# A PSUM pool of its own for the second layer's attention, with one two-bank score buffer and a lead of two units

## The chip, the cores and the metric

The kernel runs on one core of a Trainium2 chip. The metric is device time in microseconds (us), the median of several runs. One further execution is taken by the hardware profiler; its trace is what is read below. Engines are named as the profile names them: PE is TensorE (PEld its weight loads), DVE VectorE, ACT ScalarE, POOL GpSimd, SP the queue that issues the loads.

## The reference, cut to what matters

A trunk of two layers on x of 512 x 1024 floats. The first is a latent-attention layer with softmax, the second a stick-breaking-attention layer that reads keys and values made from the residual stream after the first. Each layer's mixer output is multiplied by a SiLU gate, projected and added to the stream; then a per-layer embedding, gated by a sigmoid of the stream, is added. The part that the change touches:

```python
def sb_layer(x, k_sh, v_sh, ln_g, w_in, w_out):
    h = rmsnorm(x, ln_g)
    q, gate = jnp.split(h @ w_in, [MIX_WIDTH], axis=-1)
    ...
    o = stick_breaking_attention(q, k_sh, v_sh)
    return x + (o * jax.nn.silu(gate)) @ w_out

# in stick_breaking_attention, for a block of 128 queries:
z = einsum(q, k) * scale
log_one_minus = where(mask, log_sigmoid(-z), 0)
tail = reversed_cumsum(log_one_minus) - log_one_minus
a = where(mask, exp(log_sigmoid(z) + tail), 0)
o = einsum(a, v)
```

The kernel uses products in place of sums of logarithms: sigmoid(z) times the running product of sigmoid(-z).

## The kernel before

Every fp32 operand of a product is split into a rounded high part and the rest, and each product is three TensorE products (`mm3`, L122 to L124). A weight tile is loaded by SP, for the second layer multiplied by norm gains on POOL (L170, L606), its high part cast on ACT (L131), its low part subtracted on DVE or POOL (L132).

PSUM has eight banks of 128 x 512 floats. One pool, `pp`, serves the whole kernel with tags `g` (2 banks), `s` (2), `t` (3) and `o` (1). `gps` takes the bank of a weight product from a string of tags in turn: "gst" for the first group of each layer, "gstt" for the embedding and the output projection, "g" alone while attention runs.

The order of instructions on each engine is drawn up when the kernel is built. A list scheduler goes by a priority number, which is the place in the program unless it is shifted, and by a simulated timeline: of what is ready it takes the lowest number. `hp(offset=...)` moves instructions ahead by so many steps, `pri(self.mp)` moves the products of `gemm_gen` and `sb_group` back by so many. A tag's slots are given out in that order; a tile that finds none free waits for the release of an old one. A pool opened where a closed one lay waits, by default, with all its tiles for every user of the closed one.

The first layer's attention takes 64 units (16 heads, 4 query blocks). `mla_front` makes a unit's scores, and its DVE instruction at L574 writes an SBUF tile of tag `e`; exponential, normalisation (L582, L585) and four units later the transposes (L532, in `pt_evac`) follow, after which the `e` tile is free. The tile of query block 0 is kept until block 1's transposes. The same tag holds the input's eight x tiles and four tiles of `out_ple`.

Between the layers, `out_ple` ends with the gate products of eight chunks, and for each a sigmoid (L744), a product (L746), a sum (L747), its split into the two parts of x2 (L148, L149), a square (L875) and a sum of squares on POOL (L876). From the last sum come eight tiny products (L881), the mean (L884), the power -1/2 (L885), and `row_of`: four transposes (L190) and the copy to R2 (L192).

In the second layer heads go in four groups of four. For each group `sb_group` makes V (four tiles of 24 products of 256 columns), two chunks of K and two of Q (24 products of 512 columns each). While the attention of a group runs, the generator in `windows` makes the next group's, then the SiLU gates (`gate2`).

A pair of heads has three units (u = 0, 1, 2), so there are 24. `sb_scores` writes each head's scores to a bank of its own; the two heads sit on the upper and the lower 64 rows of the array. `sb_front` makes four sigmoids (L648, L653), a scan per head on DVE (L658) and a product per head on POOL (L659). `pt_evac` transposes the result on PE (L532) and copies it out in two parts (L537, L538); after a pair's third unit `av` (L552) multiplies with V. `sb_layer` puts the transposes `lead` units behind the scores.

Of the kernel before, what the change touches and what calls it, by code (L numbers as in the profile page):

```python
# [6 lines left out]
F32 = mybir.dt.float32  # L7
# [3 lines left out]
AF = mybir.ActivationFunctionType  # L11
# [33 lines left out]
SB_LEAD = 1  # L45
# [3 lines left out]
SB_PRIO = (0, 100, 0, 100)  # L49
MLA_FILL = (0, 100)  # L50
SB_FILL = (0, 300)
# [7 lines left out]
SPREAD_PLE = "gstt"  # L59

# [19 lines left out]
def trunk_kernel(tc, A):  # L80
    from contextlib import ExitStack
    with ExitStack() as ctx:
        Trunk(ctx, tc, A).run()


class Trunk:
    def __init__(self, ctx, tc, A):
        self.tc, self.nc, self.A = tc, tc.nc, A
        self.cp = ctx.enter_context(tc.tile_pool(name="cp", bufs=1))
        self.sp = ctx.enter_context(tc.tile_pool(name="sp", bufs=1))  # L90
        self.pp = ctx.enter_context(tc.tile_pool(name="pp", bufs=1, space=PSUM))
        self.dp = ctx.enter_context(tc.tile_pool(name="dp", bufs=1, space=DRAM))
        self.n = 0

    BUFS = {"A": 8, "B": 10, "qk": 8, "hat": 6, "gate": 8, "v": 2, "f": 6, "e": 12, "ws": 3, "wh": 2, "wl": 2, "R": 1,
            "sm": 16, "smg": 3, "g": 2, "s": 2, "t": 3, "o": 1}
# [529 lines left out]
    def sb_scores(self, u, qs, ks):  # L626

        nc = self.nc
        ps = [self.ps([P, S], "s") for _ in range(2)]
        parts = [(1, 0, 2), (0, 2, 2)] if u == 0 else [(u + 1, 0, u + 2)]  # L630
        terms = [(qs[0], ks[0]), (qs[0], ks[1]), (qs[1], ks[0])]
        for j, c0, nb in parts:
            for i, (q, k) in enumerate(terms):
                for hh in range(2):
                    rows = slice(hh * HD, (hh + 1) * HD)
                    nc.tensor.matmul(ps[hh][:, c0 * P:(c0 + nb) * P], lhsT=q[rows, j * P:(j + 1) * P],  # L636
                                     rhs=k[rows, 0:nb * P], start=i == 0, stop=i == 2, tile_position=(hh * HD, 0))
        return ps

    def sb_front(self, u, ps):  # L640


        nc, v = self.nc, self.nc.vector
        n = (3, 3, 4)[u] * P
        mask = self.maskp if u == 0 else self.maskb[:, S - n:S]
        oms, bs = [[self.t([P, S + 8], F32, "e") for _ in range(2)] for _ in range(2)]
        for om, p in zip(oms, ps):
            nc.scalar.activation(om[:, 0:n], p[:, 0:n], AF.Sigmoid, scale=-(HD ** -0.5))  # L648
            v.memset(om[:, n:n + 1], 0.0)
            if u == 0:  # L650
                v.memset(om[:, 2 * P - 1:2 * P], 0.0)
        for b, p in zip(bs, ps):
            nc.scalar.activation(b[:, 0:n], p[:, 0:n], AF.Sigmoid, scale=HD ** -0.5)  # L653
            if u == 0:
                v.memset(b[:, 2 * P - 1:2 * P], 0.0)
        for om, b in zip(oms, bs):
            x = om[:, 0:n][:, ::-1]
            v.tensor_tensor_scan(out=x, data0=x, data1=mask[:, ::-1], initial=0.0, op0=ALU.mult, op1=ALU.max)  # L658
            nc.gpsimd.tensor_tensor(out=b[:, 0:n], in0=b[:, 0:n], in1=om[:, 1:n + 1], op=ALU.mult)  # L659
        return bs  # L660

    def sb_layer(self, windows, pair, lead, off):
# [5 lines left out]
        for i in range(NU * NH // 2 + lead):  # L668
# [13 lines left out]
            if b >= 0:  # L682
                m, u = divmod(b, NU)
                e = bs.pop(b)
                with hp(offset=off[2]):
                    for hh in range(2):
                        self.pt_evac(2 * m + hh, u, e[hh])
# [110 lines left out]
    def run(self):  # L798
# [88 lines left out]
        self.R2 = self.row_of(r2)  # L887
        self.gates, self.outs, self.og = [[None] * NK for _ in range(3)]
# [18 lines left out]
        self.cyc = SPREAD  # L907
# [10 lines left out]
        self.cyc = SPREAD_PLE  # L918
# [63 lines left out]
```

## Time and profile before

| | |
|---|---|
| median of 3 runs | 714.16 us (713.75 to 715.67) |
| the profiled execution | 718.74 us |
| its span, first to last instruction | 717.0 us |
| PE busy | 681.0 us (95%) |
| DVE, ACT, POOL busy | 497.1, 387.8, 364.0 us |
| mean granted clock | 0.98 |

The times of rows are us from the start of the span. A row of a timeline gives start, duration, engine, line and operation, output and inputs; in brackets the engine's idle time before it and what ended that. A busy matmul row includes its passage through the array, so rows overlap: from start to start is the rate. In a windows row the busy times stand in the order PE, PEld, DVE, ACT, POOL, unless it is of one engine; then come the granted clock, the share of the DMA engines and GB/s.

### The profile page before, as it was taken

The page shows a single profiled execution, that of the slowest core. Times are in us where ns is not written, and L with a number is a line of the kernel's source. Part 1 is how long each engine was busy: PE and PEld are TensorE (multiplying, and loading weights), DVE is VectorE, ACT ScalarE, POOL GpSimd, SP SyncE. Part 2 cuts the span into 40 slices and gives each one's busy share as a digit, 9 for nine tenths or more (in the row PEclk, how much of TensorE's full clock was granted, in tenths as well). Part 3 has the DMA queues.
Part 4 walks back from the last instruction along what each step waited for, and adds up shares of the span by engine and source line. Part 5 has one row for each costly group of instructions (what it writes and reads, how often), then busy time and mean ns, then how long its engine had stood idle before and what let it go on. Part 6 is the DMA issues. An engine that isn't in the chain of part 4 may idle for free.

```text
span 717.0 us, 10008 instructions
## 1 busy us (share of the span) xinstructions
PE 681.0 (95%) x3558; PEld 570.6 (80%) x3558; DVE 497.1 (69%) x935; ACT 387.8 (54%) x773; POOL 364.0 (51%) x293
## 2 busy tenths in 40 slices
PE   8799999999988999999799999999999989999997
PEld 6588888878867888887688888877788768888886
DVE  6748499989877865645757787776976987644432
ACT  7256596966986865453343665543563545622321
POOL 6629566754894441038635655545843895200132
PEclk9999999999999999999999999999999999999999
DMA  6242211000014212533322122033012211443231
GB/s 230 67 130 87 79 49 63 30 31 16 16 44 134 89 59 73 159 119 109 128 89 89 51 68 60 1 88 89 30 59 88 89 59 59 161 137 112 75 134 59
DMA packets 21474, 59.29 MB, mean 83 GB/s; under 512 B 2864, under 2 KB 3376, under 8 KB 21424
## 3 DMA queue, kind: packets, MB, share of 16 engines
q1 hardware_dynamic: 21424, 58.65, 25.9%
q8 instruction: 28, 0.46, 0.3%
q14 instruction: 22, 0.18, 0.1%
HBM read 54.45 MB, written 4.19 MB: 82 GB/s over the span
## 4 chain that ended last, share of the span: by engine, by line
PE 59%; DVE 14%; issue 11%; POOL 8%; ACT 6%; DMA 1%; SPq 0%; POOLq 0%; ACTq 0%; DVEq 0%
PE g L122 10%; PE g L124 10%; PE g L123 10%; PE o L552 4%; PE t L122 3%; PE t L124 3%; PE t L123 3%; PE s L122 3%; PE s L123 3%; PE t L532 3%; PE s L124 3%; PE s L636 2%; POOL e L659 2%; DVE wl L132 1%; POOL ws L170 1%
## 5 line engine op out<-in xcount | busy, mean ns | idle before, releaser
L131 ACT CAST wh<-ws 128x1024 fp32r<-128x1024 f32 (+2 forms) x92 | 90.7, 986 | 137.0 <-issue 53.1
L132 DVE TENSOR_TENSOR wl<-ws,wh 128x1024 fp32r<-128x1024 f32 (+2 forms) x72 | 100.1, 1391 | 42.3 <-ACT wh L131 41.9
L122 PE MATMUL g<-A,wh 128*128 128x512 f32 x280 | 113.0, 403 | 9.2 <-ACT wh L331 4.6
L123 PE MATMUL g<-A,wh 128*128 128x512 f32 x280 | 112.2, 401 | 1.6 <-DVE A L149 1.6
L124 PE MATMUL g<-A,wl 128*128 128x512 f32 x280 | 111.2, 401 | 1.2 <-DVE wl L132 0.8
L659 POOL TENSOR_TENSOR e<-e,e 128x384 f32<-128x384 f32 (+1 forms) x48 | 63.3, 1337 | 31.8 <-ACT e L653 11.3
L170 POOL TENSOR_TENSOR ws<-ws,gc 128x1024 f32<-128x1024 f32 x24 | 53.3, 2220 | 51.4 <-DMA ws<-in_w_k 22.7
L122 PEld LDWEIGHTS g<-A,wh 128*128 128x128 f32 x280 | 53.6, 192 | 21.1 <-ACT wh L331 5.7
L537 ACT CAST pth<-t 128x384 fp32r<-128x384 f32 (+1 forms) x96 | 48.4, 525 | 36.5 <-PE t L532 34.3
L538 DVE TENSOR_TENSOR ptl<-t,pth 128x384 fp32r<-128x384 f32 (+1 forms) x96 | 55.4, 591 | 15.9 <-ACT pth L537 15.5
L746 POOL TENSOR_TENSOR f<-f,B 128x512 f32<-128x512 f32 x8 | 14.2, 1773 | 102.1 <-ACT f L744 101.9
L124 PEld LDWEIGHTS g<-A,wl 128*128 128x128 f32 x280 | 53.2, 191 | 13.4 <-DVE wl L132 1.5
L123 PEld LDWEIGHTS g<-A,wh 128*128 128x128 f32 x280 | 53.7, 192 | 12.6 <-DVE A L149 2.0
L532 PE MATMUL t<-ident,e 128*128 128x128 f32 x320 | 55.7, 275 | 7.8 <-POOL e L659 6.6
L132 POOL TENSOR_TENSOR wl<-ws,wh 128x1024 fp32r<-128x1024 f32 (+2 forms) x20 | 41.6, 2079 | 25.1 <-ACT wh L131 24.3
L532 PEld LDWEIGHTS t<-ident,e 128*128 128x128 f32 x320 | 39.0, 140 | 15.2 <-POOL e L659 8.7
L658 DVE TENSOR_TENSOR_SCAN e<-e,maskb 128x384 f32<-128x384 f32 (+1 forms) x32 | 44.7, 1431 | 9.0 <-ACT e L648 8.9
L578 ACT ACTIVATE e<-e,sm,smg 128x128 f32<-128x128 f32 (+1 forms) x64 | 42.1, 660 | 11.6 <-DVE sm L577 11.3
L582 POOL TENSOR_SCALAR e<-e,sm 128x384 f32<-128x384 f32 (+3 forms) x48 | 29.1, 615 | 25.9 <-DVE sm L580 24.4
L552 PE MATMUL o<-pth,v 128*128 128x256 f32 (+2 forms) x128 | 42.1, 340 | 0.0
L552 PE MATMUL o<-ptl,v 128*128 128x256 f32 (+2 forms) x128 | 41.2, 343 | 0.0
L648 ACT ACTIVATE e<-s 128x384 f32<-128x384 f32 (+1 forms) x48 | 23.4, 525 | 31.7 <-PE s L636 31.5
(320 smaller groups left out, 1857.1 us busy)
## 6 DMA issues: line engine op xcount, KB each, us to landing
ws<-in_w_pg SPq DMA_DIRECT2D x16, 512.0 KB, 3.5
ws<-in_w_g SPq DMA_DIRECT2D x8, 512.0 KB, 3.2
ws<-in_w_o SPq DMA_DIRECT2D x16, 256.0 KB, 2.6
ws<-in_w_v SPq DMA_DIRECT2D x8, 512.0 KB, 3.6
ws<-in_w_k SPq DMA_DIRECT2D x8, 512.0 KB, 3.5
ws<-in_w_sq SPq DMA_DIRECT2D x8, 512.0 KB, 3.5
ws<-in_w_sg SPq DMA_DIRECT2D x8, 512.0 KB, 3.5
ws<-in_w_o SPq DMA_DIRECT2D x8, 512.0 KB, 3.5
```

The costliest lines, as they stand in the source:

```text
L122: mm(ps, lhsT=wh, rhs=xh, start=first, stop=False)
L123: mm(ps, lhsT=wh, rhs=xl, start=False, stop=False)
L124: mm(ps, lhsT=wl, rhs=xh, start=False, stop=last)
L131: nc.scalar.copy(out=wh, in_=src)
L132: lo_engine.tensor_tensor(out=wl, in0=src, in1=f32(wh), op=ALU.subtract)
L170: nc.gpsimd.tensor_tensor(out=ws, in0=ws, in1=gain.unsqueeze(2).to_broadcast((P, nk, P)), op=ALU.mult)
L532: nc.tensor.transpose(ps[:, i], src[:, c * P:(c + 1) * P], self.ident)
L537: nc.scalar.copy(out=views[0], in_=ps)
L538: nc.vector.tensor_tensor(out=views[1], in0=ps, in1=f32(views[0]), op=ALU.subtract)
L552: nc.tensor.matmul(ps[:, q0:S], lhsT=V[:, c, hh], rhs=rhs, start=(c == 0 and i == 0), stop=(c == NT - 1 and i == 1))
L658: v.tensor_tensor_scan(out=x, data0=x, data1=mask[:, ::-1], initial=0.0, op0=ALU.mult, op1=ALU.max)
L659: nc.gpsimd.tensor_tensor(out=b[:, 0:n], in0=b[:, 0:n], in1=om[:, 1:n + 1], op=ALU.mult)
```

## The change

The second layer gets a PSUM pool of its own, opened after R2 is made and the first pool closed. Its tags are `g` (2 banks), `t` (3), `o` (1) and `s2`, one buffer of two banks. Both heads' scores are one tile of that tag; the sigmoids take both heads at once, and `e` tiles hold both heads (6 slots of twice the size in place of 12). Scores go two units ahead of transposes. All priority offsets of the layer become zero. Weight products of the layer's first group, of the embedding and of the output projection take banks by "gtt".

```diff
@@ -42,13 +42,13 @@
 
 MLA_LEAD = (4, 4, 2)
 
-SB_LEAD = 1
+SB_LEAD = 2
 
 
 MLA_PRIO = (50, 50, 50, 50)
-SB_PRIO = (0, 100, 0, 100)
+SB_PRIO = (0, 0, 0, 0)
 MLA_FILL = (0, 100)
-SB_FILL = (0, 300)
+SB_FILL = (0, 0)
 
 
 GATES = (4, 1, 1, 2, 0)
@@ -57,6 +57,7 @@
 
 SPREAD = "gst"
 SPREAD_PLE = "gstt"
+SPREAD_SB = "gtt"
 
 
 def _two_pi_parts():
@@ -78,9 +79,10 @@
 
 
 def trunk_kernel(tc, A):
-    from contextlib import ExitStack
     with ExitStack() as ctx:
-        Trunk(ctx, tc, A).run()
+        t = Trunk(ctx, tc, A)
+        with t.pctx:
+            t.run()
 
 
 class Trunk:
@@ -88,12 +90,13 @@
         self.tc, self.nc, self.A = tc, tc.nc, A
         self.cp = ctx.enter_context(tc.tile_pool(name="cp", bufs=1))
         self.sp = ctx.enter_context(tc.tile_pool(name="sp", bufs=1))
-        self.pp = ctx.enter_context(tc.tile_pool(name="pp", bufs=1, space=PSUM))
+        self.pctx = ExitStack()
+        self.pp = self.pctx.enter_context(tc.tile_pool(name="pp", bufs=1, space=PSUM))
         self.dp = ctx.enter_context(tc.tile_pool(name="dp", bufs=1, space=DRAM))
         self.n = 0
 
-    BUFS = {"A": 8, "B": 10, "qk": 8, "hat": 6, "gate": 8, "v": 2, "f": 6, "e": 12, "ws": 3, "wh": 2, "wl": 2, "R": 1,
-            "sm": 16, "smg": 3, "g": 2, "s": 2, "t": 3, "o": 1}
+    BUFS = {"A": 8, "B": 10, "qk": 8, "hat": 6, "gate": 8, "v": 2, "f": 6, "e": 6, "ws": 3, "wh": 2, "wl": 2, "R": 1,
+            "sm": 16, "smg": 3, "g": 2, "s": 2, "t": 3, "o": 1, "s2": 1}
 
     def t(self, shape, dt, tag):
         self.n += 1
@@ -626,14 +629,14 @@
     def sb_scores(self, u, qs, ks):
 
         nc = self.nc
-        ps = [self.ps([P, S], "s") for _ in range(2)]
+        ps = self.ps([P, 2, S], "s2")
         parts = [(1, 0, 2), (0, 2, 2)] if u == 0 else [(u + 1, 0, u + 2)]
         terms = [(qs[0], ks[0]), (qs[0], ks[1]), (qs[1], ks[0])]
         for j, c0, nb in parts:
             for i, (q, k) in enumerate(terms):
                 for hh in range(2):
                     rows = slice(hh * HD, (hh + 1) * HD)
-                    nc.tensor.matmul(ps[hh][:, c0 * P:(c0 + nb) * P], lhsT=q[rows, j * P:(j + 1) * P],
+                    nc.tensor.matmul(ps[:, hh, c0 * P:(c0 + nb) * P], lhsT=q[rows, j * P:(j + 1) * P],
                                      rhs=k[rows, 0:nb * P], start=i == 0, stop=i == 2, tile_position=(hh * HD, 0))
         return ps
 
@@ -643,21 +646,18 @@
         nc, v = self.nc, self.nc.vector
         n = (3, 3, 4)[u] * P
         mask = self.maskp if u == 0 else self.maskb[:, S - n:S]
-        oms, bs = [[self.t([P, S + 8], F32, "e") for _ in range(2)] for _ in range(2)]
-        for om, p in zip(oms, ps):
-            nc.scalar.activation(om[:, 0:n], p[:, 0:n], AF.Sigmoid, scale=-(HD ** -0.5))
-            v.memset(om[:, n:n + 1], 0.0)
-            if u == 0:
-                v.memset(om[:, 2 * P - 1:2 * P], 0.0)
-        for b, p in zip(bs, ps):
-            nc.scalar.activation(b[:, 0:n], p[:, 0:n], AF.Sigmoid, scale=HD ** -0.5)
-            if u == 0:
-                v.memset(b[:, 2 * P - 1:2 * P], 0.0)
-        for om, b in zip(oms, bs):
-            x = om[:, 0:n][:, ::-1]
+        om, b = [self.t([P, 2, S + 8], F32, "e") for _ in range(2)]
+        nc.scalar.activation(om[:, :, 0:n], ps[:, :, 0:n], AF.Sigmoid, scale=-(HD ** -0.5))
+        nc.scalar.activation(b[:, :, 0:n], ps[:, :, 0:n], AF.Sigmoid, scale=HD ** -0.5)
+        v.memset(om[:, :, n:n + 1], 0.0)
+        if u == 0:
+            for x in (om, b):
+                v.memset(x[:, :, 2 * P - 1:2 * P], 0.0)
+        for hh in range(2):
+            x = om[:, hh, 0:n][:, ::-1]
             v.tensor_tensor_scan(out=x, data0=x, data1=mask[:, ::-1], initial=0.0, op0=ALU.mult, op1=ALU.max)
-            nc.gpsimd.tensor_tensor(out=b[:, 0:n], in0=b[:, 0:n], in1=om[:, 1:n + 1], op=ALU.mult)
-        return bs
+            nc.gpsimd.tensor_tensor(out=b[:, hh, 0:n], in0=b[:, hh, 0:n], in1=om[:, hh, 1:n + 1], op=ALU.mult)
+        return b
 
     def sb_layer(self, windows, pair, lead, off):
 
@@ -684,7 +684,7 @@
                 e = bs.pop(b)
                 with hp(offset=off[2]):
                     for hh in range(2):
-                        self.pt_evac(2 * m + hh, u, e[hh])
+                        self.pt_evac(2 * m + hh, u, e[:, hh])
                 if u == NU - 1:
                     with hp(offset=off[3]):
                         for hh in range(2):
@@ -885,6 +885,8 @@
         nc.gpsimd.tensor_tensor(out=r2, in0=r2, in1=self.mhalf.to_broadcast((P, NT)), op=ALU.pow)
         self.r2 = r2
         self.R2 = self.row_of(r2)
+        self.pctx.close()
+        self.pp = self.pctx.enter_context(self.tc.tile_pool(name="pq", bufs=1, space=PSUM))
         self.gates, self.outs, self.og = [[None] * NK for _ in range(3)]
         self.groups = [[] for _ in range(NG)]
         self.out_tag = "gate"
@@ -904,7 +906,7 @@
                 self.gated(m)
 
         grp = lambda g: self.sb_group(g, self.groups[g])
-        self.cyc = SPREAD
+        self.cyc = SPREAD_SB
         for _ in grp(0):
             pass
         self.cyc = "g"
@@ -915,7 +917,7 @@
         self.part = {}
         self.wp, self.mp = SB_FILL
         self.sb_layer(windows, pair2, SB_LEAD, SB_PRIO)
-        self.cyc = SPREAD_PLE
+        self.cyc = SPREAD_SB
         self.wp, self.mp = 0, 0
         for _ in self.pp_gemm(1):
             pass
```

## Rows read from the trace of the kernel before

**Rows 1.** The page's part 1, the line of TensorE.

```profile
PE 681.0 (95%) x3558; PEld 570.6 (80%) x3558; DVE 497.1 (69%) x935; ACT 387.8 (54%) x773; POOL 364.0 (51%) x293
```

**Rows 2.** Windows of two stages: busy us (x instructions) by engine, granted clock, DMA.

```profile
440.00:480.00 40.00, 37.90 (x232) 32.34 (x232) 32.44 (x53) 21.84 (x44) 22.95 (x15) 0.96 0.17 42
560.00:611.00 51.00, 47.25 (x237) 36.77 (x236) 41.91 (x55) 29.08 (x53) 42.33 (x27) 0.97 0.23 73
```

**Rows 3.** Waits of PE, 363 to 611 us: total, times, longest.

```profile
PE t L532 <- POOL e L659: 6.6, 6, 2.3
```

**Rows 4.** Timeline of POOL: start, duration, line, operation, idle time before.

```profile
571.22 2.82 POOL L170 TENSOR_TENSOR ws<-ws,gc 128x1024 f32<-128x1024 f32 x1
577.53 3.77 POOL L659 TENSOR_TENSOR e<-e,e 128x512 f32<-128x512 f32 x2
```

**Rows 5.** Timeline of PE: two products at full clock, then after a wait.

```profile
385.26 0.39 PE L123 MATMUL s<-A,wh 128*128 128x512 f32 x1
385.49 0.39 PE L124 MATMUL s<-A,wl 128*128 128x512 f32 x1
...
579.65 0.66 PE L532 MATMUL t<-ident,e 128*128 128x128 f32 x4 [2.31 <-POOL e L659]
...
583.20 0.63 PE L123 MATMUL g<-A,wh 128*128 128x512 f32 x1
```

**Rows 6.** Timeline of PE: scores (L636) apart, and six together.

```profile
444.77 0.96 PE L636 MATMUL s<-B,qk 64*128 64x512 f32 x3
445.66 0.39 PE L123 MATMUL g<-wl,A 128*128 128x256 f32 x1
445.97 0.96 PE L636 MATMUL s<-B,qk 64*128 64x512 f32 x3
446.86 0.39 PE L124 MATMUL g<-wh,A 128*128 128x256 f32 x1
...
461.91 0.28 PE L124 MATMUL g<-wh,A 128*128 128x256 f32 x1
462.03 0.28 PE L122 MATMUL g<-wh,A 128*128 128x256 f32 x1
462.24 0.97 PE L636 MATMUL s<-B,qk 64*128 64x512 f32 x6
```

**Rows 7.** Groups by line and form of ScalarE, 386 to 611 us.

```profile
L648 ACT ACTIVATE e<-s 128x384 f32<-128x384 f32 x32 | 14.3, 489 | 16.6 <-PE s L636 16.4
```

**Rows 8.** Timeline of PE between the layers.

```profile
344.33 0.39 PE L124 MATMUL s<-qk,wl 128*128 128x512 f32 x1
...
357.31 0.58 PE L122 MATMUL g<-wh,A 128*128 128x256 f32 x1 [2.36 <-ACT A L148]
```

**Rows 9.** Timelines of four engines: the chain from the last gate to R2.

```profile
350.25 0.58 ACT L744 ACTIVATE f<-s 128x512 f32<-128x512 f32 x1
352.52 1.77 DVE L746 TENSOR_TENSOR f<-f,v 128x512 f32<-128x512 f32 x1
354.33 2.27 DVE L747 TENSOR_TENSOR f<-f,e 128x512 f32<-128x512 f32 x1
357.16 0.63 ACT L875 ACTIVATE f<-f 128x512 f32<-128x512 f32 x1
357.93 1.28 POOL L876 TENSOR_TENSOR f<-f,f 128x512 f32<-128x512 f32 x1 [1.87 <-ACT f L875]
362.23 0.95 PE L881 MATMUL o<-ones,f 128*128 128x1 f32 x8
363.88 1.02 POOL L885 TENSOR_TENSOR r<-r,mhalf 128x4 f32<-128x4 f32 x1 [4.68 <-DVE r L884]
369.85 0.58 ACT L192 COPY R<-o 128x512 f32<-128x512 f32 x1
```

**Rows 10.** Windows to 207 us: L574's records on DVE, then L532's products.

```profile
0.00:207.00 207.00, 22.61 (x96) 0.97 0.22 72
...
0.00:207.00 207.00, 19.06 (x100) 12.70 (x100) 0.97 0.22 72
```

More of the change, by code (lines that the diff above doesn't have):

```diff
@@ L1 @@
-from contextlib import contextmanager
+from contextlib import ExitStack, contextmanager
 import concourse.bass as bass
```

## The prediction

> **What bounds the kernel now.** I read the page's engine line first: TensorE is busy 95% of the span [rows 1], so time can only come out of its idle stretches and out of slow spots in its stream. The windows by stage, read next, show where those lie in the second layer: from 440 to 480 us and from 560 to 611 us PE is not full, and the mean granted clock is 0.96 and 0.97 [rows 2]. The waits of PE between 363 and 611 us come next: the largest by far is of transposes (L532) on GpSimd's product (L659), 6.6 us in 6 waits [rows 3]. The reason is in GpSimd's own queue: at 571 us it multiplies a weight tile by its gains (2.82 us), then come two products of gates, and only at 577.53 does it reach the product that PE needs, 3.77 us for the two heads [rows 4]; PE starts its transposes 2.31 us late, and soon after the granted clock is at the 1.2 GHz level for a while: a 512-column product's row reads 0.63 us at 583.20, and 0.39 at 2.4 GHz, where one starts every 0.23 us (385.26 to 385.49) [rows 5]. Last I read the stretch between the layers (344 to 386 us), where the new pool begins.
>
> **The change, part by part.**
>
> *Lead of two, all priorities zero.* A unit's transposes now stand two units behind its scores, with two units' worth of weight products between. The 6.6 us [rows 3] have that distance to vanish in: a unit of the layer takes some 9 us (386 to 611 us over 24 units), the worst lateness is 2.3. Taking the fill products out of their 300-step delay also spreads the attention units, which now come in bursts, over the whole layer, and with them GpSimd's load (42 of 51 us in the last burst [rows 2]). I take 6.0 of the 6.6. The two drops of the clock cost (1 - 0.96) x 40 = 1.6 us and (1 - 0.97) x 51 = 1.5 us [rows 2]; each follows such a wait, and I take one of them as gone, 1.6. Bounds: nothing to 9.7 us for waits and clock together. What the order may bring instead is a wait of its own, since nothing holds the weight products back any more until their weights are split: between 0 and the 6.6 us that the old order had, and I take 2.4, nearer to the low end because PE has products of several units and chunks to choose from, and a late weight stops only its own.
>
> *One two-bank score tile.* Now the two heads' score products write two tiles. The first bank comes free one sigmoid earlier than the second, and in 6 of 24 units the two heads are issued apart: three products at 444.77, one weight product, three at 445.97, and the next thing starts at 446.86. Where six stand together (462.24) the pairs run side by side on the two halves of the array's rows and take 0.97 us together, as long as three alone [rows 6]. From 444.77 to 446.86 are 2.09 us; less the weight product's usual 0.12 and the 0.97 this is 1.0 lost. One tile makes the six ready at once. Sum of the six: 6.0 us; I take 5, bounds 0 and 6.
>
> Here the Trainium skill has a rule (TensorEngine Tiling (Array Packing), Key Properties): a change of tiling mode drains the engine. In this trace the single weight product between two score runs took 0.31 us from start to start (445.66 to 445.97) where 0.12 is usual (461.91 to 462.03) [rows 6]. Going by the rule alone, each of the six units saves two mode changes of about 0.2, or 2.4 us in all, estimated; the rows give 6, because most of the loss is the lost pairing.
>
> *Sigmoids and memsets.* Four sigmoids a unit become two of twice the width. At 489 ns for 384 columns [rows 7] this saves at most two instructions' fixed part, below 0.5 us a unit, on ScalarE, which is busy 54% and never the last to finish in the layer. Nothing, covered by the weight products; without that cover it would be a gain of that size. Fewer memsets on VectorE: nothing, likewise. One buffer instead of two halves does not shorten the time until the next unit's scores may begin, since both halves had to be read before, too.
>
> *Closing the first pool.* This is the dear part. The new pool lies on the same eight banks, and by default a pool waits for every user of the pool that it replaces; the last user is the copy of R2 (L192), which comes at the end of the norm's chain. Now PE goes from the last gate product (344.33) straight into group 0's products: 96 of 256 columns at 0.12 us and 96 of 512 at 0.23, or 11.5 + 22.1 = 33.6 us of work, the last of which starts at 385.49 and gives way at 385.7 [rows 5, 6, 8]. It needs 41.2 us for them, because it waits on x2's last chunks (2.36 us of idle time before 357.31, and two shorter waits) and then runs at the low clock for a while, but most of the chain is covered. After the change nothing covers it. The chain: sigmoid at 350.25, product and sum on VectorE to 356.6, square, sum on GpSimd to 359.21, the eight tiny products (0.95), power (1.02), transposes, copy (0.58) [rows 9]. In the old order the last four are spread out, from 362.23 to 370.4, since PE and the others have other things to do; run back to back from 359.2, with 0.75 for L884 and the transposes together and 0.25 at each of five hand-overs (my estimates, from the 0.95 of the eight tiny products and the steps of the chain that follow each other now), R2 is ready at 363.7. Group 0 then ends at 363.7 + 33.6 + 1.6, for one more drop of the clock at the price of those above, = 398.9, against 385.7 before: **+13.2 us**. Bounds: if all of the chain ran without queueing, from 344.7 with these durations, R2 would come at some 355.8 and the loss be 5.3; if the last steps stay as spread out as they are, it comes at 370.4 and the loss is 19.9. I keep 13.2, since none of what queues before it (weight multiplications and splits) is touched.
>
> *Tile "e" from 12 single to 6 double slots.* The first layer uses the same tag with tiles of single width, so it loses half its slots. At 207 us VectorE had begun 48 of its 64 units (each leaves two records) and PE had done the ten transposes of each of 10 heads, 40 units: 8 tiles lived [rows 10]. Of 64 units 15 begin with more than six alive, eight or fewer each time. With six slots the start of these would slip, by 0.1 to 3.3 us except for two at 205 us (7.6 and 6.9); and nearly all have more room than that between normalisation and transpose. Only units 18, 19 and 34 have not (2.5, 1.9 and 1.1 us). Bounds -2 (a reshuffled order can also come out better) to +6; I take +1. The input stage has eight x tiles on that tag too; their loads slip behind the first squares, some 0 to 0.5, in the same +1.
>
> *Banks "gtt" in place of "gst" and "gstt".* Five banks for streams whose chunks take 24 x 0.23 = 5.5 us each on PE and under 2 us to evacuate. Nothing; PE covers it, and it would show as a wait of L122 on an evacuation.
>
> Sum: +13.2 + 1 - 6.0 - 1.6 - 5 + 2.4 = **+4.0 us**. The profiled execution took 718.74 us for a span of 717.0, 4.6 above the median of the runs, 714.16. I add the difference to the median: 714.16 + 4.0 = **718.2**.
>
> **The rivals.**
>
> *Faster: the boundary is cheap.* For it: the chain's bare durations add up to only 11 us of the 19 that PE would stand idle; a schedule that is drawn anew may put it ahead of weight preparation. Against it: those preparations are ready earlier than the chain's steps, as now. With R2 at 355.8 the sum is 4.0 - 7.9 = -3.9, or 710.3; with all of the 6.6 + 3.1 + 6.0 us of the second layer recovered too and no new wait, 5.3 + 1 - 15.7 = -9.4, or 704.8. It decides from R2 ready before 357.6 us on the old clock of events, where the sum passes -2.1.
>
> *The first layer pays for "e".* If the slips pass into PE (VectorE is the busiest engine there beside PE), +5 to +7 in place of +1: 722 to 724. Against it: the room between normalisation and transpose.
>
> *One score buffer serialises.* Unit i+1's scores wait for two wide sigmoids, about 2 us (four times 489 ns [rows 7]); if a quarter of the 24 units pay it, no weight product being ready in between, this is +12, or 730, and 724 if half of it is covered. Against it: before, too, the two banks belonged to one unit. The Trainium skill (Trainium Kernel Development and Optimization, Best Practices) advises to double-buffer, there for transfers; carried over to this buffer it speaks for the rival, and no run here shows such a wait.
>
> *The close holds nothing back.* If the new pool's tiles waited only for their own banks, the 13.2 would be under 1 and the time 705 to 706. The pools' default speaks against it.
>
> **How the numbers follow.** A measurement of this kernel can tell about 0.3%, 2.1 us, from no change. Forecast as summed, 714 to 722 us: 0.47 (of it 0.12 within 0.3%). Cheap boundary, 704 to 713: 0.28 (0.05 within). First layer: 0.15 (0.02 within). Serialised scores: 0.08. Close without effect: 0.02, faster. So faster 0.25, same 0.19, slower 0.56. Range 707 to 727: below it lie the better part of the last case and the far end of the cheap boundary (0.09), above it most of the serialised scores and the tail of the first layer (0.10).
>
> **What would show it.** Right: PE without a product for 15 to 20 us before R2's copy, then group 0 dense; transposes that hardly wait on L659; scores always six or twelve together; PE's waits in the first layer about as before. Wrong: group 0's products before the copy, or the copy early, which means 710 or less; new waits of L636 on sigmoids or of L122 to L124 on weight splits above 5 us, which mean 722 or more.

## The result, and the profile after

The changed kernel takes **738.48 us**, the median of 4 runs (736.19 to 740.26); the kernel before took 714.91 beside it (713.75 to 717.95). The ratio is 1.0328, 95% interval 1.0287 to 1.0368: slower by 23.6 us. Slower was forecast, but by 4.0 us; 738.5 lies above the range of 707 to 727. The profiled execution took 737.92 us for a span of 736.1.

The page's engine line answers to [rows 1].

```profile
PE 695.3 (94%) x3558; PEld 570.5 (78%) x3558; DVE 492.1 (67%) x895; ACT 382.6 (52%) x725; POOL 351.8 (48%) x293
```

PE has 3558 instructions as before, yet is busy 14.3 us longer (681.0 in [rows 1]). So a part of the loss is no wait at all: the same products take longer. Where, is read by cutting both spans at the first score product (386.0 us before, 391.2 after). First the kernel before, then the changed one; the columns after the busy times are the granted clock, the DMA share and GB/s.

```profile
0.00:386.00 386.00, 361.51 (x1856) 306.82 (x1856) 275.97 (x618) 234.33 (x503) 210.09 (x200) 0.97 0.27 86
386.00:717.00 331.00, 319.48 (x1703) 263.82 (x1702) 221.12 (x318) 153.50 (x271) 153.87 (x93) 0.99 0.25 79
```

```profile
0.00:391.20 391.20, 359.41 (x1856) 303.05 (x1856) 276.27 (x618) 233.11 (x503) 210.34 (x200) 0.97 0.26 85
391.20:736.10 344.90, 335.91 (x1703) 267.44 (x1702) 215.81 (x278) 149.53 (x223) 141.50 (x93) 0.98 0.24 76
```

Up to the first score 5.2 us are lost, from there to the end 13.9. In the second stretch PE's idle time fell, from 11.5 to 9.0 us, while its busy time grew by 16.4.

The first stretch holds two things that nearly cancel. PE's timeline between the layers, of the changed kernel (beside [rows 8]):

```profile
334.84 0.39 PE L127 MATMUL s<-qk,wl 128*128 128x512 f32 x1
...
349.60 1.87 PE L881 MATMUL o<-ones,f 128*128 128x1 f32 x8 [14.38 <-POOL f L876]
352.82 1.11 PE L193 MATMUL o<-ident,r 128*128 128x128 f32 x4 [1.35 <-POOL r L885]
354.61 0.58 PE L125 MATMUL g<-wh,A 128*128 128x256 f32 x1 [0.67 <-ACT R L195]
...
390.67 0.39 PE L127 MATMUL t<-A,wl 128*128 128x512 f32 x1
...
391.22 0.50 PE L639 MATMUL s<-B,qk 64*128 64x256 f32 x4
```

The last gate product starts at 334.84 us where it was 344.33 [rows 8]: the first layer is 9.5 us shorter. Then PE has nothing for 14.4 us, until the norm's chain ends, and group 0 begins only behind R2's copy (L195). From the last gate product to the first score it is 56.4 us where it was 41.7, 14.7 more. The granted clock was 0.50 from 339.0 to 359.4 us, the 1.2 GHz level, after PE had stood idle since 335, so group 0's first products run at it too. Its steps, of ScalarE, GpSimd and VectorE, beside [rows 9]:

```profile
347.52 0.62 ACT L875 ACTIVATE f<-f 128x512 f32<-128x512 f32 x1
353.97 0.58 ACT L195 COPY R<-o 128x512 f32<-128x512 f32 x1 [5.82 <-PE o L193]
```

```profile
348.29 1.26 POOL L876 TENSOR_TENSOR f<-f,f 128x512 f32<-128x512 f32 x1 [1.87 <-ACT f L875]
351.75 1.02 POOL L885 TENSOR_TENSOR r<-r,mhalf 128x4 f32<-128x4 f32 x1 [2.20 <-DVE r L884]
```

The waits of PE from 340 to 600 us (total, times, longest) answer to [rows 3]. The wait of the transposes (now L535) for GpSimd's product, 6.6 us before, is gone.

```profile
PE o L881 <- POOL f L876: 14.4, 1, 14.4
PE t L535 <- DVE ptl L541: 2.2, 4, 0.8
PE o L193 <- POOL r L885: 1.3, 1, 1.3
PE o L555 <- DVE ptl L541: 1.2, 1, 1.2
PE g L125 <- ACT R L195: 0.7, 1, 0.7
PE t L127 <- DVE wl L135: 0.5, 1, 0.5
PE s L639 <- ACT e L651: 0.3, 1, 0.3
```

What the second stretch pays for stands in no view of waits. It is seen in PE's timeline where attention and weights meet (beside [rows 6]):

```profile
413.95 0.51 PE L126 MATMUL g<-A,wh 128*128 128x512 f32 x1
414.38 0.38 PE L639 MATMUL s<-B,qk 64*128 64x256 f32 x1
414.69 0.49 PE L127 MATMUL g<-A,wl 128*128 128x512 f32 x1
...
419.11 0.50 PE L127 MATMUL g<-A,wl 128*128 128x512 f32 x1
...
441.25 0.51 PE L639 MATMUL s<-B,qk 64*128 64x256 f32 x1
441.69 0.58 PE L125 MATMUL g<-wh,A 128*128 128x256 f32 x1
442.20 0.58 PE L639 MATMUL s<-B,qk 64*128 64x256 f32 x1
442.71 0.58 PE L126 MATMUL g<-wl,A 128*128 128x256 f32 x1
```

Score products (64 rows) and weight products (128 rows) go one by one in turn. Seven such pairs fill 413.95 to 419.11, 0.74 us a pair. Counted in PE's timeline, the 192 score products stand in 75 separate runs, 51 of them of a single product; before there were 36 runs, none of them single. With the priorities at zero, scores, fill products (the weight products that are made while attention runs), transposes and averages stand at the same place in the scheduler's order, and it deals them out in turn. The score products' group shows the price: first the kernel before, then the changed one (busy us, mean ns).

```profile
L636 PE MATMUL s<-B,qk 64*128 64x256 f32 (+2 forms) x192 | 30.5, 350 | 0.0
```

```profile
L639 PE MATMUL s<-B,qk 64*128 64x256 f32 (+2 forms) x192 | 41.1, 386 | 0.3 <-ACT e L651 0.3
```

Soon after 441 us the granted clock falls too, with PE never idle by its rows (which include the passage through the array); windows of the changed kernel, the last two beside [rows 2]:

```profile
441.00:460.00 19.00, 19.00 (x85) 14.79 (x84) 5.81 (x14) 4.88 (x9) 3.54 (x3) 0.69 0.09 28
440.00:480.00 40.00, 38.92 (x208) 29.94 (x207) 24.39 (x44) 19.33 (x33) 12.43 (x11) 0.83 0.08 26
560.00:611.00 51.00, 49.96 (x230) 36.56 (x228) 35.65 (x39) 21.39 (x30) 32.15 (x19) 1.00 0.26 82
```

### The profile page after: what moved, and what is told of

Its sections match the earlier page's. It is cut to its first block, busy times and chain, and to the rows that moved or that the text cites. A ratio compares the mean times of both kernels' runs of the same rounds, so it can differ in the third digit from the quotient of the medians.

```text
span 736.1 us, 9978 instructions
## 1 busy us (share of the span) xinstructions
PE 695.3 (94%) x3558; PEld 570.5 (78%) x3558; DVE 492.1 (67%) x895; ACT 382.6 (52%) x725; POOL 351.8 (48%) x293
## 4 chain that ended last, share of the span: by engine, by line
PE 64%; DVE 17%; issue 11%; ACT 3%; POOL 3%; DMA 1%; SPq 0%; ACTq 0%; POOLq 0%; DVEq 0%
PE g L125 11%; PE g L126 11%; PE g L127 11%; PE t L127 5%; PE t L125 5%; PE t L126 5%; PE o L555 4%; PE s L639 4%; PE t L535 3%; DVE e L658 2%; DVE ptl L541 2%; DVE A L152 2%; PE s L125 1%; DVE e L577 1%; PE s L126 1%
## 5 line engine op out<-in xcount | busy, mean ns | idle before, releaser
L135 DVE TENSOR_TENSOR wl<-ws,wh 128x1024 fp32r<-128x1024 f32 (+2 forms) x72 | 101.6, 1411 | 38.5 <-ACT wh L134 38.3
L125 PE MATMUL g<-A,wh 128*128 128x512 f32 x288 | 115.7, 402 | 4.5 <-ACT wh L334 4.5
L126 PE MATMUL g<-A,wh 128*128 128x512 f32 x288 | 114.9, 399 | 1.0 <-DVE A L152 0.9
L127 PE MATMUL g<-A,wl 128*128 128x512 f32 x288 | 113.9, 400 | 0.6 <-POOL wl L335 0.6
L173 POOL TENSOR_TENSOR ws<-ws,gc 128x1024 f32<-128x1024 f32 x24 | 48.1, 2004 | 69.1 <-DMA ws<-in_w_sq 26.2
L659 POOL TENSOR_TENSOR e<-e,e 128x384 f32<-128x384 f32 (+1 forms) x48 | 56.5, 1195 | 50.0 <-DVE e L655 17.0
L746 POOL TENSOR_TENSOR f<-f,B 128x512 f32<-128x512 f32 x8 | 14.1, 1766 | 110.8 <-ACT f L744 110.6
L126 PEld LDWEIGHTS g<-A,wh 128*128 128x128 f32 x288 | 54.1, 188 | 14.3 <-DVE A L152 2.7
L127 PEld LDWEIGHTS g<-A,wl 128*128 128x128 f32 x288 | 54.1, 188 | 13.2 <-POOL wl L335 1.0
L535 PE MATMUL t<-ident,e 128*128 128x128 f32 x320 | 57.9, 279 | 3.5 <-DVE ptl L541 2.4
L540 ACT CAST pth<-t 128x384 fp32r<-128x384 f32 (+1 forms) x96 | 48.0, 520 | 22.1 <-PE t L535 14.7
L535 PEld LDWEIGHTS t<-ident,e 128*128 128x128 f32 x320 | 39.3, 142 | 11.9 <-issue 6.2
L658 DVE TENSOR_TENSOR_SCAN e<-e,maskb 128x384 f32<-128x384 f32 (+1 forms) x32 | 40.5, 1307 | 10.1 <-ACT e L650 10.1
L639 PE MATMUL s<-B,qk 64*128 64x256 f32 (+2 forms) x192 | 41.1, 386 | 0.3 <-ACT e L651 0.3
```

The source lines that it names most:

```text
L125: mm(ps, lhsT=wh, rhs=xh, start=first, stop=False)
L126: mm(ps, lhsT=wh, rhs=xl, start=False, stop=False)
L127: mm(ps, lhsT=wl, rhs=xh, start=False, stop=last)
L135: lo_engine.tensor_tensor(out=wl, in0=src, in1=f32(wh), op=ALU.subtract)
L173: nc.gpsimd.tensor_tensor(out=ws, in0=ws, in1=gain.unsqueeze(2).to_broadcast((P, nk, P)), op=ALU.mult)
L535: nc.tensor.transpose(ps[:, i], src[:, c * P:(c + 1) * P], self.ident)
```

## The experiments

The **theory** after this reading: three separate sums that add up, the boundary (about +14 us), fewer e slots (a gain in the first layer), and the dealing out of score products (above 20 us). The **rivals**: the extra time of the second layer comes from the late start, the single score buffer or the lead; the idle time of the boundary is only shifted. Times are medians; kernels were run in four sets (e1 to e4, e5 to e8, e9 to e11, e12), the changed kernel in one of its own. The median of the kernel before was 717.8, 715.4, 714.2 and 715.2 in the four and 714.9 in that one, so that differences of 2 to 3 us between kernels of different sets tell nothing. Ratios are to the kernel before of the same set, with their 95% interval.

| run | median us | ratio |
|---|---|---|
| e1 old priorities | 710.83 | 0.9895 [0.9845, 0.9944] |
| e2 waits by tile | 734.58 | 1.0225 [1.0175, 1.0275] |
| e3 before, priorities zero | 749.56 | 1.0413 [1.0345, 1.0481] |
| e4 before, six e slots | 712.29 | 0.9925 [0.9899, 0.9952] |
| e5 old priorities, no boundary | 696.71 | 0.9733 [0.9693, 0.9773] |
| e6 old priorities, lead 1 | 711.93 | 0.9946 [0.9923, 0.9968] |
| e7 before, six e slots, lead 2 | 711.80 | 0.9963 [0.9930, 0.9996] |
| e8 priorities zero, no boundary | 724.62 | 1.0117 [1.0073, 1.0161] |
| e9 as changed, 128-row scores | 717.10 | 1.0042 [1.0021, 1.0063] |
| e10 as e1, 128-row scores | 713.65 | 0.9991 [0.9965, 1.0016] |
| e11 as e8, fill's offset back | 697.22 | 0.9756 [0.9716, 0.9797] |
| e12 before, five e slots | 712.39 | 0.9947 [0.9910, 0.9983] |

**e1: the old priorities in the changed kernel.**

```diff
-SB_PRIO = (0, 0, 0, 0)
+SB_PRIO = (0, 100, 0, 100)
-SB_FILL = (0, 0)
+SB_FILL = (0, 300)
```

> The changed kernel with the old priority offsets of the second layer (0, 100, 0, 100 and 0, 300), all else as changed. Theory A, broken score runs: with all offsets zero, scores, weight products and transposes get the same priority numbers (a block under an offset gives the number back at its end), so the scheduler deals them out one by one; each step between 64-row and 128-row products costs about 0.2 us and the heads no longer run in pairs. Then the old offsets take PE's score runs from 74 back to about 30 and the time falls by 13 to 20 us, to 719 to 725. Theory B, the single two-bank buffer and the lead of two are what costs: the runs may change, but the time stays within 5 us of 738.

Measured 710.83 us, 27.7 under the changed kernel (31 by the ratios) and 8 below what theory A gave; the offsets alone turn a loss into a small gain. The first score comes at 391.4 us, as in the changed kernel, so the late start is not the cause. Score products now stand in 28 runs, none of them single. Their group, and the stretch from the first score to the end:

```profile
L639 PE MATMUL s<-B,qk 64*128 64x256 f32 (+2 forms) x192 | 22.9, 350 | 0.0
```

```profile
391.40:709.30 317.90, 308.84 (x1703) 256.02 (x1702) 223.08 (x278) 148.79 (x223) 150.41 (x93) 1.00 0.25 82
```

The stretch is 27.0 us shorter, PE's idle time in it 9.1 us where the changed kernel has 9.0: all of the difference is busy time.

**e3: zero priorities in the kernel before.**

```diff
-SB_PRIO = (0, 100, 0, 100)
+SB_PRIO = (0, 0, 0, 0)
-SB_FILL = (0, 300)
+SB_FILL = (0, 0)
```

> The kernel before with nothing but the second layer's priority offsets set to zero: one pool, two one-bank score tiles, lead of one. Theory A: score runs of one product each, as in the changed kernel or more, and 13 to 22 us more than before, 728 to 737. Theory B: alternation of 64-row and 128-row products is cheap, the time is within 4 us of 715.

749.56 us, some 32 us above the kernel before and more than theory A gave (728 to 737). The zero offsets cost about as much without the new pool, buffer and lead: the score buffer and the lead are not needed for the loss. Here there are 105 runs of score products, 74 of them single.

**e9 and e10: the same dealing without a change of rows.** In the changed kernel (e9) and in e1 (e10) each score product takes all 128 rows of q and k.

```diff
-  nc.tensor.matmul(ps[:, hh, ...], lhsT=q[rows, j * P:(j + 1) * P],
-      rhs=k[rows, 0:nb * P], ..., tile_position=(hh * HD, 0))
+  nc.tensor.matmul(ps[:, hh, ...], lhsT=q[:, j * P:(j + 1) * P],
+      rhs=k[:, 0:nb * P], ...)
```

> The new kernel, offsets zero, dealt out one by one as in the new kernel (75 separate runs), but each score product takes all 128 rows of q and k where it took the 64 of one head: this changes what is computed (both heads' products summed), the number of products and their columns are the same. To be read against the same edit with the old offsets, sent with it. Theory (what the dealing costs is the change between products of 64 and of 128 rows): without the change of rows the dealing costs little; this run and the other are within 6 us of each other, both near 700 to 715 us, and score and weight products in turn take 0.1 to 0.25 us each. Rival (any change of operands between two products costs it, or the order itself, with its later scores): this run stays 18 to 28 us above the other, 725 to 740 us.

> The run before this one with the old priority offsets (28 separate runs of score products), full 128 rows in each score product, so with both heads' products summed. Score products of 64 rows ran two at a time (8.9 us for the 96 of 256 columns with the old offsets), those of 128 rows can not, so the 192 products take an estimated 28 us at the rate of the weight products where they took 22.9 us; the 56 changes of rows go. Theory: 700 to 712 us, and the run with offsets zero within 6 us of it. Rival: 712 to 720 us, with the run with offsets zero 18 to 28 us above it.

717.10 and 713.65 us, each some 2 us above its theory's range, but within 6 of each other: with 128-row scores the dealing costs 3.5 us, where it costs 27.7 with 64-row ones. e9 has the runs of the changed kernel (75, 51 single), its boundary and its columns, and is 21.4 us faster. Its timeline, at the place shown above:

```profile
412.58 0.40 PE L126 MATMUL g<-A,wh 128*128 128x512 f32 x1
412.81 0.28 PE L639 MATMUL s<-B,qk 128*128 128x256 f32 x1
412.93 0.40 PE L127 MATMUL g<-A,wl 128*128 128x512 f32 x1
...
415.05 0.40 PE L127 MATMUL g<-A,wl 128*128 128x512 f32 x1
```

Seven pairs take 2.47 us, 0.35 a pair, where 64-row ones took 0.74: two changes of rows cost 0.38 us, one 0.19. The clock is whole as well; e9, from the first score to the end:

```profile
389.80:713.90 324.10, 314.92 (x1704) 270.81 (x1702) 216.02 (x278) 149.40 (x223) 142.82 (x93) 1.00 0.25 80
```

e1, with 64-row scores in long runs, has 1.00 as well. So in these traces the low clock of the changed kernel goes with the two together, 64-row scores and their dealing, and not with the order alone. It is worth (1 - 0.98) x 344.9 = 6.9 us. The 47 runs more than in e1 are 47 x 0.38 = 17.9 us. Together 24.8 of the 27.0. But 56 score products, those left over in runs of odd length, have also lost their partner on the other half of the rows: some 4 us, estimated from 0.12 us for 256 and 0.23 for 512 columns. With that the parts are 2 us above what was measured, so the split among them is rough.

**e5 and e8: no boundary.** Only the score banks lie in a pool that is closed and replaced; the banks g, t and o live through. With the old priorities (e5) and with zero (e8):

```diff
+        self.pp = ctx.enter_context(tc.tile_pool(name="pp", ...))
-        self.pp = self.pctx.enter_context(tc.tile_pool(name="pp", ...))
+        self.sc = self.pctx.enter_context(tc.tile_pool(name="pscore", ...))
...
-        return self.pp.tile(...)
+        return (self.sc if tag in ("s", "s2") else self.pp).tile(...)
...
-        self.pp = self.pctx.enter_context(self.tc.tile_pool(name="pq", ...))
+        self.sc = self.pctx.enter_context(self.tc.tile_pool(name="pq", ...))
```

> The new kernel with the old priority offsets, and only the score banks' pool closed and opened anew at the layer boundary; the banks of all other products live through. Theory (the boundary costs its own time, about 15 us of TensorE standing still, because group 0's V products stand behind R2's transposes): the last first-layer gate product at about 335 us, the first V product within 3 us of it, first score near 377 us, and the whole 12 to 15 us under the 710.8 of the run with the old offsets alone: 696 to 699 us. Rival (TensorE's idle time there is only shifted: group 0's evacuations, which need r2, stall it as long a little later, or the weights' transfers do): 706 to 711 us, with the missing time as new waits within the first 40 us of the second layer.

> The new kernel, offsets zero, with only the score banks' pool closed and opened at the boundary: the boundary alone is undone, the score products stay dealt out one by one (75 separate runs). Theory (boundary and dealing are two separate costs that add): the wait of 14.4 us goes and the rest stays, 721 to 726 us, the second layer from first score to end 340 to 347 us as in the new kernel. Rival (the boundary's wait is given back later, or the dealing only hurts after a late start): 733 to 738 us, or under 715 us.

e5: 696.71 us, 14.1 under e1. e8: 724.62, 13.9 under the changed kernel. These pairs are of different sets; by the ratios they are 11.6 and 15.1. The traces agree: from the last gate product to the first score it is 41.7 and 42.0 us in e5 and e8, as in the kernel before (41.7), and 57.0 and 56.4 in e1 and the changed kernel. So the boundary costs some 14 us whatever the priorities are, and of it only 1 to 2 us are given back later (from the first score to the end e5 takes 1.3 us more than e1, e8 2.1 more than the changed kernel): boundary and dealing add. PE's timeline of e5 (line numbers one higher) shows the first V product right behind the last gate product, and R2's chain under group 0:

```profile
334.02 0.39 PE L128 MATMUL s<-qk,wl 128*128 128x512 f32 x1
334.24 0.28 PE L126 MATMUL g<-wh,A 128*128 128x256 f32 x1
...
351.89 0.95 PE L882 MATMUL o<-ones,f 128*128 128x1 f32 x8
...
358.64 0.60 PE L194 MATMUL o<-ident,r 128*128 128x128 f32 x4
...
375.75 0.50 PE L640 MATMUL s<-B,qk 64*128 64x256 f32 x4
```

**e2: the new pool's waits by tile.** `reuse_waits="tile"` on the pool pq, so that a tile waits only for its own banks.

> The changed kernel, but the second pool's tiles wait only for the old users of their own banks and not for all of the first pool. If the closing of the pool costs the 13 us of the prediction's sum, PE no longer idles 14 us before the eight tiny products, and the time falls by 10 to 14 us, to 724 to 728. The rival, that the idle stretch is made up elsewhere (the weights of group 0 are ready sooner, the first layer ends sooner): the time falls by less than 5 us.

The theory fell: 734.58 us, 3.9 under the changed kernel (7 by the ratios), and PE stands idle 14.5 us before L881 as well. PE's order of products is that of the changed kernel, with the V products still behind R2's transposes. The waits did get fewer: the first V product now starts before R2's copy, where it stood behind it.

```profile
353.43 0.56 PE L125 MATMUL g<-wh,A 128*128 128x256 f32 x1
```

```profile
353.81 0.59 ACT L195 COPY R<-o 128x512 f32<-128x512 f32 x1 [5.82 <-PE o L193]
```

That is 1.2 us earlier than in the changed kernel (354.61). With fewer waits the order alone is enough to hold group 0 back; why the order comes out so even then is open. The second layer gained another 1.5 us (343.4 us from the first score to the end, against 344.9); the granted clock was 0.99 there, against 0.98, which would cover it.

**e4 and e12: six and five e slots in the kernel before**, of double width; a unit's tiles are halves of two.

```diff
-"e": 12
+"e": 6     (e12: 5)
...
-        oms, bs = [[self.t([P, S + 8], F32, "e") for _ in range(2)] for _ in range(2)]
+        oms, bs = [[x[:, hh] for hh in range(2)] for x in (self.t([P, 2, S + 8], F32, "e"), self.t([P, 2, S + 8], F32, "e"))]
```

> The kernel before with tag e as 6 slots of double width: the second layer's four tiles of a unit are halves of two, everything else as before. The changed kernel's first layer reached its last gate product 9.5 us sooner than that of before in the profiled executions. If that comes from the fewer slots (another order in the first layer), this kernel's last gate product comes at about 335 us and the time is 5 to 9 us below before, 706 to 710. If it is the spread between executions, or belongs to another edit, the time is within 3 us of before. The prediction's term was +1.

> The kernel before with five double-width e slots in place of twelve single ones, a unit's tiles as halves of two; with six such slots the first layer's last gate product came at 335.7 us instead of 344.3 and the median was 712.3. Theory (the first layer has never more than a few e tiles alive, and fewer slots only change the order in which the scheduler deals out its stages, so that the gain is one of order and not of the number of slots): the last gate product at 334 to 345 us, with no new waits for an e slot's release, 708 to 718 us. Rival (the first layer needs the slots, and five are below the point where they bind, as the prediction's term for e had it): the last gate product later than 346 us and 719 to 730 us.

712.29 and 712.39 us; by the ratios a gain of 5.4 and 3.8. The last gate product comes at 335.7 and 337.3 us, against 344.3. The windows of the stretch where most of it arises, of the kernel before and then of e4:

```profile
207.00:271.00 64.00, 57.86 (x320) 49.12 (x319) 47.16 (x119) 45.99 (x94) 33.60 (x36) 0.97 0.26 83
```

```profile
207.00:271.00 64.00, 62.39 (x343) 52.43 (x343) 47.99 (x124) 43.98 (x94) 32.79 (x35) 1.00 0.27 90
```

PE's idle time falls from 6.1 to 1.6 us here. The slots do bind a little: VectorE stands idle before L574 until transposes (L532) have freed a tile, 0.4 us in e4 (once) and 2.3 us in e12 (4 times), where the kernel before has no such wait; e12's theory had said that there would be none. PE does not lose by it; the schedule that comes out is a better one. Why it does is open: there are two counts and the old one, and a list scheduler can fall either way. Two things limit the size. e3, whose first layer is that of the kernel before, reached its last gate product at 341.3 us, so 3 of the 8.6 us lie within what twelve slots give in two executions. And part of it is the clock, as the windows from 60 to 330 us of the kernel before and of e4 show: (1 - 0.98) x 270 = 5.4 us.

```profile
60.00:330.00 270.00, 256.90 (x1363) 220.66 (x1362) 203.63 (x517) 183.73 (x411) 144.76 (x132) 0.98 0.23 73
```

```profile
60.00:330.00 270.00, 262.12 (x1398) 223.00 (x1396) 210.19 (x520) 184.68 (x414) 153.01 (x135) 1.00 0.23 76
```

In e4's second layer, though, score products stand in 47 runs (28 of three: more units split in two than before), their group takes 40.6 us, and the stretch from the first score to the end is 334.3 us, 3.4 longer.

**e6 and e7: the lead.** e6 is e1 with `SB_LEAD = 1`; e7 is e4 with `SB_LEAD = 2`, its two one-bank tiles kept.

> The new kernel with the old priority offsets and a lead of one unit instead of two: 30 separate runs of score products, as against 28 with a lead of two. Theory (the second unit of lead is what takes the transposes' waits for GpSimd's product away, 6.6 us before): these waits come back, 715 to 718 us, and the waits view names L659 again as what the transposes wait for. Rival (the paired sigmoids and the two-bank buffer shorten the path from score to product enough by themselves, the lead is worth nothing): 710 to 712 us, the same as with a lead of two.

> The kernel before with six double-width e slots and a lead of two, its two one-bank score tiles, one pool and offsets kept: 48 separate runs of score products, 27 of them of three products, as one bank of the pair comes free before the other. Theory (a lead of two saves the 6 us of transposes' waits, each further change between 64-row and 128-row products costs about 0.2 to 0.4 us): 712.3 - 6 + 20 runs more at 0.2 to 0.4 us each = 710 to 714 us. Rival (without the two-bank tile the split units cost nothing): 705 to 707 us. Rival (the lead saves nothing): 716 to 720 us.

711.93 us against e1's 710.83, and 711.80 against e4's 712.29: the lead of two is worth nothing that these sets can tell (by the ratios it gains 3.6 us in one pair and loses 2.7 in the other). The theory for e6 (715 to 718) fell. That e7 lies in its theory's range (710 to 714) is luck: the lead saved nothing, and the further runs that were to cost as much stand in e4 already, 47 against e7's 48. The waits for GpSimd's product (L659) between 340 and 600 us were 4.1 us in e6 and 3.0 in e1, and with six e slots and a lead of one (e4) already 2.3 of the 6.6. What does count is the two-bank tile: e5 against e7, both with six slots, lead two, old priorities and no boundary, is 696.71 against 711.80 (they differ in the paired sigmoids and the banks' turn, too, which no run separates). e7's score products stand in 48 runs, e5's in 28:

```profile
L636 PE MATMUL s<-B,qk 64*128 64x256 f32 (+2 forms) x192 | 41.5, 358 | 0.0
```

```profile
L640 PE MATMUL s<-B,qk 64*128 64x256 f32 (+2 forms) x192 | 22.9, 350 | 0.0
```

18.6 us less busy time in that group alone.

**e11: the smallest repair.** e8 with only the fill's offset back.

```diff
-SB_FILL = (0, 0)
+SB_FILL = (0, 300)
```

> The new kernel with only the score banks' pool closed at the boundary and only the fill's offset put back (0, 300), the four offsets of scores, transposes and averages at zero: 28 separate runs of score products. Theory (the fill's offset alone keeps the weight products out of the scores; the other offsets are worth nothing once it stands): 695 to 699 us, as with all old offsets. Rival (transposes and averages at the scores' priority are dealt out with them still): 700 to 710 us.

697.22 us, the same as e5 by the ratios (0.9756 and 0.9733): the offset of the fill products alone keeps them out of the scores; the four others do nothing more once it stands. e5 and e11 beat both kernels, by 2.4 to 2.7% against the kernel before.

## Why the prediction was right or wrong

**Right in size, half right in the mechanism: the boundary.** +13.2 us was forecast, 13.9 and 14.1 were measured (changed kernel against e8, e1 against e5). From the last gate product to R2's copy the prediction worked out 363.7 - 344.3 = 19.4 us; they are 334.84 to 354.55, 19.7. The rival "cheap boundary" is out. The prediction put the cost down to the new pool's waits for every user of the old one. e2 takes these away and gets 1.2 us back: what holds group 0 is its place in PE's order, behind R2's transposes. So "close holds nothing back" was wrong in its own sum too, which gave nearly all of the 13.2 us back once tiles waited only for their own banks. That replacing all the banks brings this order, and replacing the score banks alone does not, is shown by e5 and e8.

**Wrong, and decisive: *Lead of two, all priorities zero*.** The step asked what the new order might do only in waits: "a wait of its own [...] between 0 and the 6.6 us that the old order had, and I take 2.4". The waits in fact fell. What the order brought is busy time, 27.0 of the 27.7 us between the changed kernel and e1: the offsets had kept fill products out of the scores. No rival had it, so the range could not hold the time. The price stood in the rows: a weight product between two score runs took 0.31 us in place of 0.12 [rows 6]. The prediction used it for the six splits that the change removes and not for those that it adds. There the Trainium skill's rule (TensorEngine Tiling (Array Packing), Key Properties), that a change of tiling mode drains the engine, was weighed on one side only; e9 against the changed kernel agrees with it, at 0.19 us a change.

**Wrong in sign: tile "e".** +1 us was forecast, bounds -2 to +6; by e4's ratio it is -5.4 us, and -8.6 us at the last gate product (-5.6 beside e3's). The slots bind on VectorE, as the prediction had it, but a late unit was taken to delay PE. The reshuffled order, mentioned with -2, decided. At 207 us VectorE is behind (92 records of L577, beside 96 of L574 in [rows 10]), PE is not (100 transposes of L535); windows to 207 us of each:

```profile
0.00:207.00 207.00, 21.62 (x92) 0.98 0.23 73
```

```profile
0.00:207.00 207.00, 18.35 (x100) 12.36 (x100) 0.98 0.23 73
```

**Right mechanism, hidden and under-sized: one two-bank tile.** -5 us was forecast for six split units at 1.0 us. Under the old priorities it is worth 15.1 (e7 to e5), the paired sigmoids and the turn of the banks included. The price of one split fits: e7 has 27 runs of three, or some 13.5 split units, as the six slots alone split more units than the old order did. In the changed kernel the gain doesn't show: of its 75 runs of score products 51 are single, so the dealing breaks up the joined units again.

**The waits for GpSimd and the clock.** L535's wait on L659 is gone, as forecast (-6.0), but PE's idle time from the first score on fell only by 2.5 us: 2.2, 1.2 and other waits on VectorE's copies took their place. The lead had less part in it than the slots (2.3 us of this wait are left in e4 with a lead of one, 2.4 in e7 with two). Of the clock, one drop was to vanish (-1.6); at 580 us it did, and the dealing brought new ones worth 6.9.

**Right: no serialising.** L639 waits 0.3 us for the sigmoids, where that rival had 12 us. The double-buffer advice that was weighed there (the Trainium skill, Trainium Kernel Development and Optimization, Best Practices) did not bind for this buffer, by those 0.3 us. The paired sigmoid took 813 ns for both heads' 384 columns (two of 489 before [rows 7]), off the path.

```profile
L650 ACT ACTIVATE e<-s 128x768 f32<-128x768 f32 x15 | 12.2, 813 | 25.5 <-PE s L639 25.5
```

The measured sum, each step a pair of runs: six slots -5.4, two-bank tile and boundary with a lead of one -0.4 (e4 to e6; of it the boundary +14, so some -14 for the tile), lead -1.1 (e6 to e1), priorities +27.7: +20.8 us, against +23.6 measured. The 2.8 left are within the spread of the sets; by the ratios the same steps are -5.4, +1.5, -3.6 and +31.0, so each is known to some 3 us.

## What to carry to other kernels

Before priorities are levelled, ask what they keep apart: where products of 64 and of 128 rows share PE, count the runs and price each change (here 0.19 us, and the clock besides), since no view of waits shows it. Carry a price found in a row to what a change adds as well as to what it removes. When a pool has to be replaced in mid-kernel, close only the banks that change shape: some 14 us at the boundary were the price of closing the others.

## What the runs showed that was not expected

A change between 64-row and 128-row products cost 0.19 us here (0.74 against 0.35 us for a pair). The granted clock fell to 0.69 in a window in which PE was busy 19.00 of 19.00 us by its rows, with no wait ahead of it in the timeline since 431 us; just before, from 438 us on, single 64-row scores and single transposes had gone in turn. From 441.5 to 451.5 us it was 0.50, the 1.2 GHz level, and a weight product of 256 columns started every 0.21 us (446.37 to 446.58) where 0.12 is usual [rows 6]. In e9, with the same order in 128 rows, it stayed at 1.00. And a smaller buffer count made the first layer 7 to 9.5 us shorter than in the profiled execution before (4 to 6.5 beside e3's), by a better order and the clock that went with it, as far as the runs show.
